# Up-projections of two MLPs as 2x2 block products in seven block multiplications instead of eight

## The chip, the cores and the metric

The kernel runs on one core of one Trainium2 chip. The metric is the device time of one launch in microseconds. The kernel before took 1144.09 us, the median of three runs (1143.23 to 1144.69).

## What is computed

A decoder trunk of four sub-layers on x of 1 x 512 x 1024, in float32: an mLSTM mixer, an MLP, a short gated convolution, an MLP. RMS norms stand before and after each sub-layer, and the result is added to the residual stream.

```python
def layer(x, g, mixer):                  # for each of the four sub-layers
    return x + rms_norm(mixer(rms_norm(x, g_pre)), g_post)

def mlp(x, w_up, w_down):                # D_MODEL 1024, D_FF 4096
    return jnp.square(jax.nn.relu(x @ w_up)) @ w_down
```

Both MLPs have weights of their own (w_mlp_up 1024 x 4096, w_mlp_down 4096 x 1024). The other two mixers have projections of the same kind, which the change touches only in how their activations are stored.

## The kernel before

**Precision.** Every projection is done with each float32 operand split into a high and a low part of type float32r. `split` (L77) makes them: ScalarE casts the high part (L78), VectorE subtracts it from the source for the low part (L79). `mm3` (L101) then issues three matrix products on TensorE, high x high (L104), high x low (L105) and low x high (L106), all accumulated in PSUM. A block product thus needs the high part for its first two instructions, and the low part from the third on.

**Layout.** The normalised activations are turned over on TensorE (L216), four transposes to a PSUM bank, and split into xT0 and xT1. A row tile of 128 tokens is called t = 0 to 3.

**An MLP** (`mlp`, L727). The 4096 columns of the up-projection go in 32 blocks of 128. For each, one DMA brings 1024 x 128 weights (512 KB) into a raw buffer, `split` makes `w` of it, and `proj_T` (L108) does 8 x 3 products of 512 columns (all tokens) into a `pu` bank. `take` (L730) squares the rectified block: ScalarE (L732), VectorE (L734), then a split into `hb`. The first six blocks are done in halves of 256 columns, tokens 0 to 255 first, because `proj_T_many` (L137, STEPS) starts while the last tokens are still in their norm. Four blocks make a group g. `down(g)` (L750) multiplies a group with four row tiles of the down weights: 8 bank-sized results of 12 products of 512 columns. Group 0's are copied to `acc` (L774), the following ones added on VectorE (L776). The order is up, up, down(0), up, down(1) and so on; the last two groups are done together in `last_product` (L243), which also does the post-norm and the tail.

**What sets the order.** Each engine runs its instructions in the order in which they were built, and waits at the first whose operands or buffers are not ready. The builder moves instructions somewhat against the program text. SyncE (SP) issues the DMAs in the same way, in order. Steps with a long chain, the transposes of the last tokens above all, are put off by `put_off` and `step` until so many us of products have been placed ahead of them (LATE, BLOCK).

**The tail of a product** (`tail_to`, L711). `add_normed` adds the normed result to the residual (L231), `pre_norm` squares it on ScalarE (L181), takes a power on GpSimd (L173), scales it on VectorE (L207) and puts off the transposes. For tile t = 3 this chain is open when the next sub-layer's products begin.

**Buffers.** raw 2 and w 9 (weights), hb 8 pairs, xr 4 (the residual, in SBUF all the time), acc 4, xT0 and xT1 of 16 KB per partition; PSUM pu 4 banks, pd 2, pt 2.

Of the kernel before, what the change touches and what calls it, by code (L numbers as in the profile page):

```python
# [14 lines left out]
P = 128  # L15
D = 1024
# [13 lines left out]
NRAW = 2  # L30
WSPLIT = 1
NW = 9
NT2 = 8
LATE = 10.4
BLOCK = 5.2


@with_exitstack
def tile_hybrid_trunk(
# [20 lines left out]
    ps = ctx.enter_context(tc.tile_pool(name="ps", bufs=1, space=bass.MemoryType.PSUM))  # L60

# [22 lines left out]
    def load(src, a, tag="raw", bufs=NRAW):  # L84
        raw = big.tile([P, 1024], F32, tag=tag, name="raw", bufs=bufs)
        nc.sync.dma_start(raw.rearrange("p (a b) -> p a b", a=a), src)
        return raw
# [4 lines left out]
    def halved(raw, a):  # L92
        w = big.tile([P, 2, 1024], F32R, tag="w", name="w", bufs=NW)
        for hs in halves(WSPLIT):
            split(w[:, 0, hs], w[:, 1, hs], raw[:, hs])
        return w.rearrange("p s (a b) -> p s a b", a=a)
# [4 lines left out]
    def mm3(o, lhs, rhs, first, last):  # L101
        lh, ll = lhs
        rh, rl = rhs
        nc.tensor.matmul(o, lh, rh, start=first, stop=False)  # L104
        nc.tensor.matmul(o, lh, rl, start=False, stop=False)  # L105
        nc.tensor.matmul(o, ll, rh, start=False, stop=last)  # L106

    def proj_T(o, w, xT, t0, t1):  # L108
        for ko in range(KO):
            if ko % 2 == 0:  # L110
# [4 lines left out]
                (xT[0][:, t0:t1, ko, :], xT[1][:, t0:t1, ko, :]),  # L115
# [4 lines left out]
    # work for the tensor engine whose operands come through a long chain is put off until  # L120
    # enough matrix products (in us) stand before it
# [54 lines left out]
    def junk(n):  # L176
        return big.tile([P, n], BF16, tag="junk", name="junk", bufs=2)
# [7 lines left out]
    def x_tile():  # L185
        return big.tile([P, H * VA], F32, tag="xr", name="xr", bufs=4)

    def acc_tile():
        return big.tile([P, H * VA], F32, tag="acc", name="acc", bufs=4)

    def new_xT():
        return [
            big.tile([P, NT, KO, P], F32R, tag=f"xT{s}", name=f"xT{s}", bufs=1) for s in range(2)
        ]
# [4 lines left out]
    def pre_norm(t, xt, g, xT, late):  # L199
# [12 lines left out]
        def turn():  # L212
            for q, xn in enumerate(xns):
# [5 lines left out]
                hi = xT[0][:, t, 4 * q : 4 * q + 4, :].rearrange("p k n -> p (k n)")  # L219
                lo = xT[1][:, t, 4 * q : 4 * q + 4, :].rearrange("p k n -> p (k n)")  # L220
                last = split(hi, lo, tp)
# [15 lines left out]
    def hb():  # L237
        return big.tile([P, 2, S], F32R, tag="hb", name="hb", bufs=8)

    def scratch(a, b):  # L240
        return big.tile([P, a, b], F32, tag="w", name="scratch", bufs=NW)

    def last_product(wm, r0, hT, g, tail, accs=None, ends=False):  # L243
        """rows r0 : r0 + D of wm times hT, on top of accs; the post-norm's gain; then the tail"""
# [8 lines left out]
        def ks(o, t, cs, k0, k1):  # L253
            hf, c0 = divmod(cs.start, 512)
            n = cs.stop - cs.start
            for k in range(k0, k1):
# [3 lines left out]
                    (hT[k][:, 0, t * P : (t + 1) * P], hT[k][:, 1, t * P : (t + 1) * P]),  # L260
# [50 lines left out]
    # ---------------------------------------------------------------- mLSTM  # L311
    wi = w_in_mlstm[0]
    xT = new_xT()
    xs = [x_tile() for _ in range(NT)]

    def load_x(t):
        nc.sync.dma_start(xs[t][:, :D], x2[t * P : (t + 1) * P, :])

    # values, token-major, with a column of ones
# [6 lines left out]
    def v_half(hf, ws, before, after):  # L326
        for t in range(NT):
            before(t)
            o = pu()
            for ko in range(KO):  # L330
                if ko % 2 == 0:
# [3 lines left out]
                    (xT[0][:, t, ko, :], xT[1][:, t, ko, :]),  # L335
# [4 lines left out]
            if hf == 0:  # L340
                v[t] = x_tile().rearrange("p (h e) -> p h e", h=H)
                nc.gpsimd.memset(v[t][:, :, DV : DV + 1], 1.0)
# [9 lines left out]
    raws = [load(v_src(0, i), 2, "hb", 8) for i in range(2)]  # L352
    load_x(1)
    raws += [load(v_src(0, i), 2, "hb", 8) for i in range(2, 4)]

    # the first gain is spread over the partitions by a product with ones
# [7 lines left out]
    # the first tokens' way to the tensor engine goes ahead of the weights'  # L364
# [19 lines left out]
    graw = big.tile([P, KO, 2 * H], F32, tag="raw", name="graw", bufs=NRAW)  # L384
# [7 lines left out]
    # gate weights: high parts of the input gates in columns 0:4 and of the forget gates in  # L392
    # columns 32:36, their low parts 64 columns further
    gw = big.tile([P, KO, P], F32R, tag="hb", name="gw", bufs=8)
# [22 lines left out]
    for ko in range(KO):  # L417
        for part in range(2):
# [3 lines left out]
                xT[part][:, :, ko, :],  # L422
# [4 lines left out]
    def take_qk(i, o):  # L427
        h = i // 2
        if i % 2 == 0:
            qk[h] = big.tile([P, 2, S], F32, tag="hb", name="qk", bufs=8)  # L430
# [19 lines left out]
    # gates as rows [head, token]  # L450
    row_tiles = [acc_tile() for _ in range(4)]
    row_i = [0]

    def rows():
        i = row_i[0]
        row_i[0] += 1
        return row_tiles[i // 2][0:H, (i % 2) * S : (i % 2 + 1) * S]
# [58 lines left out]
    # gates as columns [token, chunk, kind, head]  # L516
# [11 lines left out]
    # chunk decays on all partitions  # L528
# [7 lines left out]
    # decay matrices exp(a_s - M_l), zero above the diagonal  # L536
# [11 lines left out]
    DT = scratch(4, S).rearrange("p h (c l) -> p h c l", c=NT)  # L548
# [26 lines left out]
    Pm = scratch(NT, S)  # L575
    kw = scratch(NT, S)
    C = [None] * H
    Cs = [big.tile([P, H, VA], F32, tag="hb", name="C", bufs=8) for _ in range(2)]

    def scores(c):  # L580
        cs = slice(c * P, (c + 1) * P)
        sp = pd()
        for h in range(H):
# [4 lines left out]
            out=Pm[:, c, :].rearrange("p (h l) -> p h l", h=H),  # L588
# [4 lines left out]
        if c < NT - 1:  # L593
            kp = pd()
            for h in range(H):
                nc.tensor.transpose(kp[:, h * P : (h + 1) * P], kT[h][:, cs], ident)
            nc.vector.tensor_tensor(
                out=kw[:, c, :].rearrange("p (h l) -> p h l", h=H),
# [5 lines left out]
    def core(c, hf):  # L604
        cs = slice(c * P, (c + 1) * P)
        if hf == 0:
            comb[c] = acc_tile().rearrange("p (h e) -> p h e", h=H)
# [253 lines left out]
```

## Time and profile before

The profiled execution:

| | value |
|---|---|
| span, first to last instruction | 1141.5 us |
| time of the runs, median | 1144.09 us |
| TensorE busy (PE) | 1130.4 us |
| VectorE busy (DVE) | 547.3 us |
| ScalarE busy (ACT) | 384.9 us |
| HBM read / written | 108.58 / 2.10 MB |

The profile is one execution. PE rows are matrix products, PEld rows weight loads beside them, SP rows DMA issues. A line such as L79 is where the instruction was issued, and where a helper issues for many callers, the tile's name tells them apart. In the groups by line, "x192 | 234.2, 1224 | 205.5" means 192 instructions, 234.2 us busy, 1224 ns for one, and 205.5 us of idle time of that engine just ahead of them, with what ended it. In a timeline the columns are start and duration in us, engine, line and operation; brackets hold the idle time before it and what released it. Listed durations of products overlap, so their rate is read from start to start.

### The profile page before, as it was taken

How to read it: one execution, taken by the hardware profiler on the slowest of the kernel's cores; microseconds unless marked ns; L12 is line 12 of the kernel's file. 1: busy time of each engine (PE TensorE's matmuls, PEld its weight loads, DVE VectorE, ACT ScalarE, POOL GpSimd, SP SyncE). 2: the span in 40 equal slices, each digit the busy share in tenths (PEclk: the TensorE clock that was granted, in tenths of full speed). 3: DMA queues.
4: the chain of work that ended last, by engine and by line, in shares of the span. 5: the costliest groups of instructions: out<-in, count | busy, mean ns of one | idle time of the engine just before them, and what ended most of it. 6: DMA issues, size and time to landing. Idle time of an engine off the chain costs nothing. (4 is left out here: it accounts for less than half of the span.)

```text
span 1141.5 us, 13204 instructions
## 1 busy us (share of the span) xinstructions
PE 1130.4 (99%) x5379; PEld 931.8 (82%) x5379; DVE 547.3 (48%) x773; ACT 384.9 (34%) x620; POOL 50.6 (4%) x85
## 2 busy tenths in 40 slices
PE   8999999999999999999999999999999999999997
PEld 6878887898888888888889888789888888888886
DVE  5643763555235344444375444355624434535423
ACT  6342542444414123133253222144532312313211
POOL 2000010100000000000130000010000000000011
PEclk9999999999999999999999999999999999999999
DMA  6512441154224224133135332205422413314201
GB/s 211 141 64 66 135 160 57 30 163 141 75 73 131 74 91 129 56 111 111 37 92 167 112 93 92 74 3 165 136 78 82 129 56 111 111 57 127 93 18 56
DMA packets 130722, 111.53 MB, mean 98 GB/s; under 512 B 4549, under 2 KB 111333, under 8 KB 130662
## 3 DMA queue, kind: packets, MB, share of 16 engines
q1 hardware_dynamic: 130662, 110.69, 31.3%
q8 instruction: 42, 0.69, 0.3%
q14 instruction: 18, 0.15, 0.0%
HBM read 108.58 MB, written 2.10 MB: 97 GB/s over the span
## 5 line engine op out<-in xcount | busy, mean ns | idle before, releaser
L79 DVE TENSOR_TENSOR w<-raw,w 128x1024 fp32r<-128x1024 f32 x192 | 234.2, 1224 | 205.5 <-ACT w L78 205.5
L78 ACT CAST w<-raw 128x1024 fp32r<-128x1024 f32 x192 | 199.7, 1049 | 379.6 <-issue 181.0
L104 PE MATMUL pu<-xT,w 128*128 128x512 f32 (+1 forms) x880 | 327.6, 372 | 0.0
L105 PE MATMUL pu<-xT,w 128*128 128x512 f32 (+1 forms) x880 | 326.3, 371 | 0.0
L106 PE MATMUL pu<-xT,w 128*128 128x512 f32 (+1 forms) x880 | 325.6, 370 | 0.0
L104 PE MATMUL pd<-w,hb 128*128 128x512 f32 (+1 forms) x648 | 253.7, 391 | 0.3 <-DVE t L278 0.2
L106 PE MATMUL pd<-w,hb 128*128 128x512 f32 (+1 forms) x648 | 253.5, 391 | 0.0
L105 PE MATMUL pd<-w,hb 128*128 128x512 f32 (+1 forms) x648 | 253.5, 391 | 0.0
L104 PEld LDWEIGHTS pu<-xT,w 128*128 128x128 f32 x880 | 165.6, 188 | 30.9 <-issue 0.6
L106 PEld LDWEIGHTS pu<-xT,w 128*128 128x128 f32 x880 | 165.5, 188 | 30.7
L105 PEld LDWEIGHTS pu<-xT,w 128*128 128x128 f32 x880 | 165.6, 188 | 30.4 <-issue 0.2
L104 PEld LDWEIGHTS pd<-w,hb 128*128 128x128 f32 x648 | 121.6, 188 | 29.0 <-DVE t L278 1.2
L105 PEld LDWEIGHTS pd<-w,hb 128*128 128x128 f32 x648 | 121.7, 188 | 27.8
L106 PEld LDWEIGHTS pd<-w,hb 128*128 128x128 f32 x648 | 121.5, 187 | 27.5
L776 DVE TENSOR_TENSOR acc<-acc,pd 128x512 f32<-128x512 f32 x80 | 54.8, 686 | 119.9 <-PE pd L106 119.9
L734 DVE SCALAR_TENSOR_TENSOR t<-pu,t 128x512 f32<-128x512 f32 x60 | 41.3, 688 | 73.7 <-ACT t L732 73.3
L732 ACT ACTIVATE t<-pu 128x512 f32<-128x512 f32 x60 | 35.8, 597 | 99.3 <-PE pu L106 99.0
L79 DVE TENSOR_TENSOR hb<-t,hb 128x512 fp32r<-128x512 f32 x80 | 54.8, 686 | 8.9 <-ACT hb L78 8.9
L78 ACT CAST hb<-t 128x512 fp32r<-128x512 f32 x80 | 49.4, 619 | 21.4 <-DVE t L734 18.1
L284 POOL TENSOR_TENSOR t<-acc,gain 128x512 f32<-128x512 f32 x14 | 18.2, 1300 | 662.6 <-DVE acc L281 347.2
L181 ACT ACTIVATE junk<-acc 128x512 bf16<-128x512 f32 (+1 forms) x17 | 10.3, 607 | 58.8 <-DVE acc L281 57.3
L281 DVE TENSOR_TENSOR acc<-acc,pd 128x512 f32<-128x512 f32 (+1 forms) x17 | 11.1, 655 | 37.3 <-PE pd L106 37.3
(139 smaller groups left out, 684.3 us busy)
## 6 DMA issues: line engine op xcount, KB each, us to landing
raw<-in_w_mlp_up_dram SPq DMA_DIRECT2D x64, 512.0 KB, 4.0
raw<-in_w_mlp_down_dram SPq DMA_DIRECT2D x64, 512.0 KB, 3.5
raw<-in_w_in_mlstm_dram SPq DMA_DIRECT2D x24, 512.0 KB, 4.1
raw<-in_w_in_conv_dram SPq DMA_DIRECT2D x24, 512.0 KB, 3.8
raw<-in_w_out_mlstm_dram SPq DMA_DIRECT2D x8, 512.0 KB, 4.0
raw<-in_w_out_conv_dram SPq DMA_DIRECT2D x8, 512.0 KB, 3.5
xr<-in_x_dram SPq DMA_DIRECT2D x7, 512.0 KB, 3.5
gain<-in_norm_g_dram SPq DMA_DIRECT2D x7, 512.0 KB, 5.0
```

Of the source, the lines that this page charges most:

```text
L78: hi = nc.scalar.copy(dst_hi, src)
L79: lo = nc.vector.tensor_tensor(out=dst_lo, in0=src, in1=dst_hi.bitcast(F32), op=ALU.subtract)
L104: nc.tensor.matmul(o, lh, rh, start=first, stop=False)
L105: nc.tensor.matmul(o, lh, rl, start=False, stop=False)
L106: nc.tensor.matmul(o, ll, rh, start=False, stop=last)
L181: nc.scalar.activation(junk(n), src, AF.Square, scale=float(D) ** -0.5, accum_out=ms[:, i : i + 1])
L281: nc.vector.tensor_tensor(out=y, in0=y, in1=o, op=ALU.add)
L284: eng.tensor_tensor(out=yg, in0=y, in1=g[:, cs], op=ALU.mult)
L732: nc.scalar.activation(r, o, AF.Relu)
L734: nc.vector.scalar_tensor_tensor(out=q, in0=o, scalar=0.0, in1=r, op0=ALU.max, op1=ALU.mult)
L776: nc.vector.tensor_tensor(out=yh, in0=yh, in1=o, op=ALU.add)
```

## The change

**Seven products.** A quad is 512 columns of the up-projection, seen as a 2x2 matrix of weight blocks a, b, c, d (each 512 x 256: a and b from the upper half of the rows, c and d from the lower), times a 2x2 matrix of activation blocks (512 features x 256 tokens). Eight quads make an MLP. In place of eight block products there are seven: X = a·a11, Z = (a+b)·p1, X += c·a12, Y = (b+d)·r3, Z += d·p4, Y += (a+d)·n2, O = (a+c)·a22. Each is 24 products of 256 columns (`prod`). Sums and differences of X, Y, Z and O give the four result blocks, five VectorE operations a quad.

**Activations.** `Seven` replaces xT0 and xT1 for the two MLPs: the seven units a11, a12, p1, r3, p4, n2 and a22, each split into high and low. a11 and a12 come of tiles 0 and 1; the others need tiles 2 and 3, with four VectorE sums for each of them. `Plain` is the layout of the other projections.

**Weights.** Each of the seven products has its own factor: a, c, d as loaded, and a+b, b+d, a+d, a+c summed on VectorE first (each sum 1024 elements per partition). Each is split, so a quad has seven splits instead of four. Its four blocks are read as 512 x 256 in runs of 1 KB. Down weights come as two row tiles of 512 columns in runs of 2 KB instead of whole rows.

**Order.** The first three quads of an MLP are begun together: three X products (`begin`), then three X += (`first_done`), then run(0), run(1), down(0), run(2), down(1), run(3) and so on. The tiles of the last tokens are put ahead with `flush`.

**Buffers.** 15 shared slots of 8 KB (tag u: weight factors, Seven, residual pairs, sums), 4 pairs hb of 16 KB, 7 raw slots of 4 KB (weight blocks, and the values of a quad), in place of the buffers above. The residual is written to DRAM (xd0 to xd3, 512 KB each) by each tile's tail, and read back when group 4's down product has been placed.

```diff
-NRAW = 2
-NW = 9
+NU = 15
+NHB = 4
+NRAW = 7
+AHEAD = 3
...
+    class Seven:
...
+        def take(self, t, q, tp):
...
+            s22, r3, p1 = temp(), temp(), temp()
+            nc.scalar.copy(s22, a)
+            tt(out=p1, in0=self.first, in1=s22, op=ALU.subtract)
+            tt(out=r3, in0=k0, in1=self.first, op=ALU.subtract)
+            self.part("p1", c, p1)
+            self.part("r3", c, r3)
+            tt(out=k0, in0=p1, in1=k0, op=ALU.subtract)
+            tt(out=k1, in0=k0, in1=k1, op=ALU.add)
...
+                pre_norm(t, xs[t], gn, nxt, LATE)
+                if aside:
+                    nc.sync.dma_start(xd[t], xs[t])
...
+        def run(self, begun):
...
+            a, b = self.block(0, 0), self.block(0, 1)
+            if not begun:
+                self.begin(a)
+            ca = self.ca
+            tt(out=a, in0=a, in1=b, op=ALU.add)
+            w = self.factor(a)
+            z = pu()
+            prod(z, w, f["p1"], True)
+            cb = self.values()
+            nc.scalar.copy(cb[:, 1], by_tile(z))
+            if not begun:
+                c = self.block(1, 0)
+                self.first_done(c)
+            d = self.block(1, 1)
+            tt(out=b, in0=b, in1=d, op=ALU.add)
+            w = self.factor(b)
+            y = pu()
+            prod(y, w, f["r3"], True)
+            nc.scalar.copy(cb[:, 0], by_tile(y))
+            w = self.factor(d)
+            tt(out=a, in0=a, in1=d, op=ALU.add)
+            w6 = self.factor(a)
+            prod(z, w, f["p4"], False)
...
+            prod(y, w6, f["n2"], False)
+            tt(out=ca[:, 1], in0=by_tile(y), in1=ca[:, 1], op=ALU.add)
...
+            prod(o, w4, f["a22"], True)
...
-        proj_T_many([(w_up[i], j * P) for j in range(2 * G)], xT, take, 6)
-        down(0)
-        for g in range(1, NG - 2):
-            up(g + 1)
-            down(g)
-        up(NG - 1)
+        flush(2)
+        quads = [quad(g) for g in range(NG)]
+        for qd in quads[:AHEAD]:
+            qd.begin()
+        for qd in quads[:AHEAD]:
+            qd.first_done()
+        flush()
+        for g in range(2):
+            quads[g].run(True)
+        for g in range(NG - 2):
+            down(g)
+            quads[g + 2].run(g + 2 < AHEAD)
+            if g == NG - 4:
+                xs[:] = token_tiles()
+                for t in range(NT):
+                    nc.sync.dma_start(xs[t], xd[t])
```

Three places show how the built order moved. Names carry a number for the buffer's use, and `out<-in` reads from right to left; `u` tiles are weight factors or activations, `raw` tiles blocks or values of a quad, `t` tiles short-lived halves.

First, TensorE at the start of the first MLP. Before, the transposes of tile 3 (t_1874, t_1876) stand in the middle of the up blocks:

```order
L104 MATMUL pu<-xT_1466,w 128x256
L105 MATMUL pu<-xT_1467,w 128x256
L106 MATMUL pu<-xT_1466,w 128x256
L216 MATMUL pt<-ident,t_1874 128x128 x4
L216 MATMUL pt<-ident,t_1876 128x128 x4
L104 MATMUL pu<-xT_1466,w 128x256
```

Of the changed kernel the same place, from the last down-type product of the mixer on; t_1785 and t_1787 are tile 2, t_1895 and t_1897 tile 3:

```order
L118 MATMUL pd<-u,hb 128x512
L278 MATMUL pt<-ident,t_1785 128x128 x4
L278 MATMUL pt<-ident,t_1787 128x128 x4
L278 MATMUL pt<-ident,t_1895 128x128 x4
L116 MATMUL pu<-u 128x256
L117 MATMUL pu<-u 128x256
L278 MATMUL pt<-ident,t_1897 128x128 x4
L118 MATMUL pu<-u 128x256
```

Tile 3's first four transposes moved from behind 90 products of the up-projection to a place ahead of all of them, and its other four to behind two.

Second, ScalarE in the middle of an MLP. Before, the reads of finished blocks (L732) alternate with casts of weights (w) for blocks five places on: w_3913 is the weight of pu_3916.

```order
L732 ACTIVATE t2_3624<-pu_3599 128x512
L78 CAST hb_3628<-t2_3626 128x512
L78 CAST w_3913<-raw_3911 128x1024
L732 ACTIVATE t2_3661<-pu_3636 128x512
L78 CAST w_3950<-raw_3948 128x1024
L78 CAST hb_3665<-t2_3663 128x512
```

Of the changed kernel, one quad; pu_3273 is X, pu_3304 Z, pu_3371 Y, u_3301 the factor a+b, u_3333 the factor c, u_3368 b+d, u_3397 d and u_3401 a+d:

```order
L81 CAST u_3301<-raw_3266 128x1024
L847 COPY raw_3298<-pu_3273 128x512
L866 COPY raw_3329<-pu_3304 128x512
L81 CAST u_3333<-raw_3331 128x1024
L81 CAST u_3368<-raw_3268 128x1024
L81 CAST u_3397<-raw_3365 128x1024
L81 CAST u_3401<-raw_3266 128x1024
L907 ACTIVATE raw_3298<-pu_3273 128x512
```

TensorE's order there is X, Z, X +=, Y, Z +=, Y +=, O. The copy of Z now stands ahead of the cast of c, the factor of X +=.

Third, VectorE early in an MLP. Before, weights' low parts (w) alternate with takes (L734) and their splits (hb):

```order
L734 SCALAR_TENSOR_TENSOR t2_2104<-pu_1914,t2_2102 128x512
L79 TENSOR_TENSOR w_2345<-raw_2343,w_2345 128x1024
L79 TENSOR_TENSOR hb_2106<-t2_2104,hb_2106 128x512
L734 SCALAR_TENSOR_TENSOR t2_2135<-pu_1915,t2_2133 128x512
L79 TENSOR_TENSOR w_2350<-raw_2348,w_2350 128x1024
L79 TENSOR_TENSOR hb_2137<-t2_2135,hb_2137 128x512
```

Of the changed kernel, from run(0)'s last factor (u_2235) to run(1)'s first (u_2307, which is a+b of raw_2302 and raw_2304):

```order
L82 TENSOR_TENSOR u_2235<-raw_2134,u_2235 128x1024
L861 TENSOR_TENSOR raw_2302<-raw_2302,raw_2304 128x1024
L885 TENSOR_TENSOR raw_1938<-pu_2175,raw_1938 128x512
L886 TENSOR_TENSOR raw_2167<-raw_1938,raw_2167 128x512
L888 TENSOR_TENSOR raw_2167<-raw_2167,raw_1938 128x512
L887 TENSOR_TENSOR raw_2167<-pu_2142,raw_2167 128x512
L910 SCALAR_TENSOR_TENSOR raw_2167<-raw_2167 128x512 x2
L893 TENSOR_TENSOR raw_1938<-pu_2266,raw_1938 128x512
L82 TENSOR_TENSOR hb_2292<-raw_2167,hb_2292 128x512 x2
L910 SCALAR_TENSOR_TENSOR raw_1938<-raw_1938 128x512
L82 TENSOR_TENSOR u_2307<-raw_2302,u_2307 128x1024
```

The sum for run(1) stands ahead of run(0)'s result sums and takes, and the low part of that same factor behind them, two of which (raw_2167 at L910 and its split) read results of run(0)'s products.

More of the change, by code (lines that the diff above doesn't have):

```diff
@@ L35 @@
 BLOCK = 5.2
+PROD = 2.86
+AHEAD = 3
 @with_exitstack
@@ L92, in halved @@
     def halved(raw, a):
-        w = big.tile([P, 2, 1024], F32R, tag="w", name="w", bufs=NW)
-        for hs in halves(WSPLIT):
-            split(w[:, 0, hs], w[:, 1, hs], raw[:, hs])
+        w = unit([2, 1024], F32R)
+        split(w[:, 0, :], w[:, 1, :], raw)
         return w.rearrange("p s (a b) -> p s a b", a=a)
@@ L183, in part_ms, with __init__, part, take @@
         )
[L185 to L194, printed above, removed]
+    class Plain:
+        def __init__(self):
+            self.f = [[unit([4, S], F32R) for _ in range(2)] for _ in range(2)]
+        def take(self, t, q, tp):
+            c = slice(t * P, (t + 1) * P)
+            return split(
+                self.f[0][q][:, :, c], self.f[1][q][:, :, c], tp.rearrange("p (k n) -> p k n", k=4)
+            )
+    class Seven:
+        def __init__(self):
+            self.f = {}
+            self.keep = [None, None]
+            self.first = None
+        def part(self, name, c, src):
+            if name not in self.f:
+                self.f[name] = unit([2, 4, 256], F32R)
+            f = self.f[name]
+            split(f[:, 0, :, c], f[:, 1, :, c], src)
+        def take(self, t, q, tp):
+            c = slice((t % 2) * P, (t % 2 + 1) * P)
+            a = tp.rearrange("p (k n) -> p k n", k=4)
+            if t < 2:
+                if t == 0:
+                    self.keep[q] = raw_tile([4, 256])
+                self.part(("a11", "a12")[q], c, a)
+                nc.scalar.copy(self.keep[q][:, :, c], a)
+                return
+            if q == 0:
+                self.first = a
+                return
+            tt = nc.vector.tensor_tensor
+            k0, k1 = (k[:, :, c] for k in self.keep)
+            def temp():
+                return half_kb().rearrange("p (k n) -> p k n", k=4)
+            s22, r3, p1 = temp(), temp(), temp()
[6 more added lines that the diff above has]
+            tt(out=k1, in0=k0, in1=k1, op=ALU.add)
+            self.part("p4", c, k1)
+            self.part("n2", c, k0)
+            self.part("a22", c, s22)
     def halves(n=2):
@@ L706, in tile_hybrid_trunk, with tail_to @@
             core((j - 1) % NT, 0 if j == 0 else 1)
-    xs = [None] * NT
-    def tail_to(gn, nxt):
+    xs = token_tiles()
+    xd = [dram.tile([P, D], F32, name=f"xd{t}") for t in range(NT)]
+    def tail_to(gn, nxt, aside=False):
         def tail(t, yg, ms2):
@@ new lines, in tile_hybrid_trunk, with prod @@
+        load_x(t)
+    xT2 = Seven()
+    last_product(w_out_mlstm[0], 0, hT, gain(0, 1), tail_to(gain(0, 2), xT2, True))
+    def prod(o, fw, fx, first):
+        for p in range(4):
+            step(PROD / 4)
+            for u in range(2):
+                mm3(
+                    o[:, u * 256 : (u + 1) * 256],
+                    [fw[:, i, p, u * P : (u + 1) * P] for i in range(2)],
+                    [fx[:, i, p, :] for i in range(2)],
+                    first and p == 0 and u == 0,
+                    p == 3,
+                )
@@ new lines, in by_tile, with quad, take @@
+    def by_tile(o):
+        return o.rearrange("p (u n) -> p u n", u=2)
+    def mlp(i, xT, gy, tail, ends=False):
+        NG = FF // P // G
+        hs = [None] * (FF // P // 2)
+        def quad(g):
+            def take(nh, half, c, o):
+                j = 2 * g + nh
+                if o is not None:
+                    nc.scalar.activation(c, o, AF.Relu)
+                else:
+                    o = c
+                nc.vector.scalar_tensor_tensor(
+                    out=c, in0=o, scalar=0.0, in1=c, op0=ALU.max, op1=ALU.mult
+                )
+                if hs[j] is None:
+                    hs[j] = pair()
+                split(hs[j][:, 0, half], hs[j][:, 1, half], c)
+            return Quad(w_up[i], g * 512, g * 512 + 256, xT, take)
+        ys = []
+        def down(g):
+            if g == 0:
+                ys.extend(token_tiles())
+            for hf, cs in enumerate(halves()):
+                ws = [
+                    piece(
+                        w_dn[i][r * P : (r + 2) * P, cs].rearrange("(k p) m -> p k m", p=P), 2
+                    )
+                    for r in (g * G, g * G + 2)
+                ]
+                for t in range(NT):
```

201 lines of the change are left out of this document (115 added, 86 removed).

## The prediction

> **What bounds the kernel now.** I read the head of the page first, then the granted clock of the core, then the view by windows.
>
> ```profile
> span 1141.5 us, 13204 instructions
> PE 1130.4 (99%) x5379; PEld 931.8 (82%) x5379; DVE 547.3 (48%) x773; ACT 384.9 (34%) x620; POOL 50.6 (4%) x85
> core 0: 1141.5 us, clock 0.998
> 360.00:420.00 60.00, 60.00 (x260) 48.56 (x259) 26.87 (x34) 16.64 (x22) 0.00 (x0) 1.00 0.31 98
> ```
>
> TensorE is busy for 99% of the span at a granted clock of 0.998. The last row is 60 us from the middle of the first MLP (busy us of PE, PEld, DVE, ACT, POOL; clock, DMA share, GB/s): PE never stops, while VectorE has 33 us free and ScalarE 43. The kernel is the sum of its matrix products, so a change wins by less product time and loses by idle time of PE. The median of the runs is 1144.09 us (1143.23 to 1144.69), 2.6 us above this span. I sum against the span and add 2.6 at the end.
>
> The price of a product is the distance from start to start in the timeline of PE, since the listed durations overlap.
>
> ```profile
> 254.74 0.28 PE L105 MATMUL pu<-xT,w 128*128 128x256 f32 x1
> ...
> 266.37 0.39 PE L104 MATMUL pu<-xT,w 128*128 128x512 f32 x1
> ...
> 277.53 0.40 PE L104 MATMUL pd<-w,hb 128*128 128x512 f32 x1
> ```
>
> Between the first two starts lie 98 products of 256 columns: 11.63/98 = 0.1187 us each. Between the second and the third lie 48 of 512 columns: 11.16/48 = 0.2325; over the down products behind them it is 0.2319, which I use.
>
> **The change: product time.** Before, an MLP's up-projection is 26 blocks of 24 products of 512 columns and 6 blocks in halves (288 products of 256): 26 x 24 x 0.2319 + 288 x 0.1187 = 178.9 us. Afterwards it is 8 quads x 7 block products x 24 products of 256 columns: 1344 x 0.1187 = 159.5 us. That takes 19.4 us off each MLP, 38.8 in all; one quad takes 19.94 us of PE instead of 4 x 24 x 0.2319 = 22.26, a gain of 2.3. The down-projections keep their products. If nothing waits, the span is 1102.7.
>
> **The change: the other engines.**
>
> ```profile
> L79 DVE TENSOR_TENSOR w<-raw,w 128x1024 fp32r<-128x1024 f32 x192 | 234.2, 1224 | 205.5 <-ACT w L78 205.5
> L78 ACT CAST w<-raw 128x1024 fp32r<-128x1024 f32 x192 | 199.7, 1049 | 379.6 <-issue 181.0 <-PE pu L106 53.5 <-DMA raw<-in_w_mlp_down_dram 53.4
> L79 DVE TENSOR_TENSOR hb<-t,hb 128x512 fp32r<-128x512 f32 x80 | 54.8, 686 | 8.9 <-ACT hb L78 8.9
> L734 DVE SCALAR_TENSOR_TENSOR t<-pu,t 128x512 f32<-128x512 f32 x60 | 41.3, 688 | 73.7 <-ACT t L732 73.3
> L774 ACT COPY acc<-pd 128x512 f32<-128x512 f32 x16 | 9.4, 587 | 27.9 <-PE pd L106 27.7
> ```
>
> A quad has seven factor splits (a cast of 1.05 us on ScalarE, then a low part of 1.22 on VectorE), four additions of 1024 elements (priced as a low part), five of 512 (0.69) and four takes (0.69 + 0.69). VectorE gets 8.6 + 4.9 + 3.4 + 5.5 = 22.4 us where it had 4 x 1.22 + 4 x 1.37 = 10.4. With the down product's 10.4 that makes 32.8 of a period of 42.2: on average it fits. The average hides which operation stands behind which, so I walked the built order with these prices and three reaction times:
>
> ```profile
> 286.09 0.59 ACT L774 COPY acc<-pd 128x512 f32<-128x512 f32 x1 [2.20 <-PE pd L106]
> ...
> 228.15 1.05 ACT L78 CAST w<-raw 128x1024 fp32r<-128x1024 f32 x1 [2.98 <-DMA raw<-in_w_mlp_up_dram]
> 229.24 1.23 DVE L79 TENSOR_TENSOR w<-raw,w 128x1024 fp32r<-128x1024 f32 x1 [1.42 <-ACT w L78]
> ...
> 252.33 0.60 ACT L732 ACTIVATE t<-pu 128x512 f32<-128x512 f32 x1 [6.71 <-PE pu L106]
> 252.82 1.04 ACT L78 CAST w<-raw 128x1024 fp32r<-128x1024 f32 x1
> ```
>
> Three groups of 12 down products after 277.53 reach 285.88, and the copy starts 0.21 later. The low part follows its cast by 0.04. From VectorE to PE I take 0.1, between the two. The last pair matters most: a cast that stands behind a read of a product on ScalarE waits for that product, 6.71 us here. It cost nothing, since its weight was for a block several products later.
>
> **Steady quads.** Now the copy of Z stands directly ahead of the cast of c (u_3333, second excerpt), which the very next product on PE needs. From Z's end: 0.21 + 0.59 for the copy + 1.05 for the cast + 0.04 + 1.22 for the low part + 0.1 = 3.2 us to the third product of X+=, less the two that need only the high part (0.24): 3.0 us idle. On VectorE the additions b+d and a+d stand behind that low part and ahead of the low part of b+d: three operations of 1.22, 3.7 us, against the 2.6 + 0.24 of products left: 0.8 idle. In the down product the third group of 512 columns needs one of two banks back from an accumulation that VectorE reaches only after the takes: about 1.0 by the walk. Together 4.7 us idle against 2.3 saved. Bounds per quad: 2.5 (only c's wait, at its shortest) and 7 (the backlog once more).
>
> **The start of an MLP.** T0 is the end of the product ahead of it; the last token tile's norm chain runs there.
>
> ```profile
> 229.79 1.04 PE L216 MATMUL pt<-ident,t 128*128 128x128 f32 x8
> ...
> 241.74 1.29 PE L216 MATMUL pt<-ident,t 128*128 128x128 f32 x8 [0.23 <-DVE t L207]
> ...
> L231 DVE SCALAR_TENSOR_TENSOR xr<-t,small,xr 128x512 f32<-128x512 f32 x31 | 22.0, 748 | 11.0 <-POOL small L173 11.0
> L207 DVE SCALAR_TENSOR_TENSOR t<-xr,small,gain 128x512 f32<-128x512 f32 x30 | 22.4, 785 | 9.4 <-POOL small L173 9.4
> L173 POOL TENSOR_TENSOR small<-small,mhalf 128x1 f32<-128x1 f32 x32 | 17.6, 550 | 193.8 <-DVE small L168 183.7 <-DVE small L172 9.7
> L181 ACT ACTIVATE junk<-xr 128x512 bf16<-128x512 f32 x32 | 20.1, 631 | 17.5 <-DVE xr L231 15.2 <-DMA xr<-in_x_dram 2.3
> ```
>
> Before, tile 3 is transposed 12 us after T0 (229.79), behind products of tiles 0 to 2 that fill all but 0.23. Afterwards its transposes stand ahead of the first product (first order excerpt), and tile 2's sums and splits stand inside its chain on VectorE. From T0: tile 2's transposes 1.0, ScalarE's copy of them 1.8; six operations of 0.69 on VectorE, 6.0; residual 0.75, 6.7; square, sum, power, 8.5; xn, 9.3; three low parts and the other xn, 12.15; low part of the first weight, 13.4. So the first begin ends at 13.5 + 22 x 0.1187 = 16.1, where 4.9 would do. Nine operations of 0.69 stand ahead of the next weight's low part: 21.2, its begin ends at 23.8. ScalarE copies that product before it casts the third weight, so the chain of 3.0 us comes again, and again ahead of the first completion: 29.5 and 35.3; the other two follow without a wait, 40.95. The work in it is 2.1 for four groups of transposes and six block products of 2.85, 19.2: **21.8 us idle**. Bounds: 16 (the last two waits covered) and 28 (the weights' transfers late by 4 and one more chain).
>
> **The first runs.** In run(0) ScalarE's copy of Z and its casts stand behind the takes of three quads: PE waits 3.6, then 0.8. Run(1) pays for the seven raw slots.
>
> ```profile
> raw<-in_w_mlp_up_dram SPq DMA_DIRECT2D x64, 512.0 KB, 4.0
> ```
>
> Its second block is issued when run(0)'s last addition (53.9) frees a slot and lands at 58.0, 4.0 later and a little. VectorE has the sum of it ahead of all of run(0)'s takes (third excerpt), and the low part behind them and the second pass of run(0)'s takes: about twelve operations of 0.69 and 1.22 later, at 67.4, where run(0) ended at 59.6. PE waits 7.7, and Y another 2.7 for a block whose slot came free late. Down(0), run(2) and down(1) add 0.3, 2.8 (an hb pair that down(0) holds) and 1.3. So 4.4 + 10.4 + 4.4 = 19.2; bounds 12 and 24.
>
> Up to down(1) this is 41 us idle. Then three quads at 4.7, quad 6 with four slots given to the reloaded residual, 6.7, and quad 7, 3.7: 24.5. An MLP has **65.5 us idle**, where before had 0.3 at these places.
>
> **Edits costed at nothing.** Four residual stores per MLP stand on SP ahead of begin's second weight; it lands by about 17.5, and ScalarE casts it at 18.9. If the stores hold the queue for longer, up to 4 us more per MLP (in the 28). The four reloads and the down pieces in 2 KB runs lie under a down product of 22 us. The other projections' layout changes addresses only: 0, from -2 to +3 for what I can't see in it.
>
> **The sum.** Per MLP 65.5 - 0.3 - 19.4 = +45.8, both +91.6: span 1233.1, time **1235.7**. Bounds of the idle per MLP: 16 to 28, 12 to 24 and five quads at 2.5 to 7: 40.5 to 87, or 1185 to 1279; the ends hardly fall together, so this case's own range is 1195 to 1270.
>
> **Rivals.** *Only the product time counts.* If the casts were ready when their products come, 38.8 us would go: **1105**. It decides where the idle of one MLP stays under 19.4 us. VectorE's 33 free us of 60 speak for it; against it, a cast behind a copy of Z can't start before Z has ended, and my start alone has 21.8. The Trainium skill ("Perfetto Trace Analysis", "Identifying the Most-Contended Engine") says to optimise the engine of highest occupancy first; by that rule PE, at 99%, gets its 38.8 us, and it leads to this rival. Chance 0.12, with partial forms up to 1140.
>
> *Only the starts cost.* If VectorE's backlog is shorter and the five later quads break even (2.3 idle each), 41 + 11.6 - 19.7 = 32.9 per MLP stay: **1210**; with starts and runs at their low ends (28), 1184. Chance 0.14.
>
> *The clock drops.* After an idle stretch PE could run slower for a while.
>
> ```profile
> 11.18 0.63 PE L104 MATMUL pu<-w,xT 128*128 128x512 f32 x1
> 11.60 0.63 PE L105 MATMUL pu<-w,xT 128*128 128x512 f32 x1
> 12.03 0.63 PE L106 MATMUL pu<-w,xT 128*128 128x512 f32 x1
> ```
>
> At the program's start products of 512 columns are 0.43 apart, not 0.232. Four us at that pace lose 1.8 us. With an idle of 8 us at an MLP's start, one of 7.7 in run(1) and two of 3 to 5 between, four such stretches per MLP add 7, both 15: **1250**; with longer slow stretches 1275. The Trainium skill ("TensorE: Matmul & The Clock Gate", "Part 1: The HAM clock gate") says that one idle window of about 3.4 us halves the clock until a busy window has passed. The start's 0.43 agrees with it; no later gap in this trace is long enough to show it. Chance 0.16.
>
> *The change doesn't do what it says*: seven block products stand in the built order, so no chance of its own.
>
> **Chances.** Forecast 0.55, clock 0.16, starts only 0.14, faster 0.12, within 0.2% 0.03 (2.3 us, about what a measurement of this kernel can tell). The range 1160 to 1275 leaves out the faster cases and thin tails.
>
> **What would show it.** Afterwards PE should be some 130 us idle; waits for ScalarE's high parts (L81) and VectorE's low parts (L82) should lead its list; each steady quad should show 3 us idle ahead of X+=, with periods of 47 us where they were 44.5; the third begin should end 29 us after T0. I am wrong if the gaps ahead of X+= are under 1 us, or if the first begin ends within 8 us of T0.

## The result, and the profile after

The changed kernel takes 1255.66 us, the median of four runs (1252.63 to 1258.14), where the kernel before took 1144.39 (four runs, 1143.23 to 1144.83). The ratio is 1.0973, with a 95% interval of 1.0951 to 1.0995. The forecast was 1235.7.

These lines are the head of the page after, and the granted clock of its core.

```profile
span 1255.6 us, 15249 instructions
PE 1145.9 (91%) x6243; PEld 985.5 (78%) x6243; DVE 733.3 (58%) x993; ACT 449.0 (36%) x692; POOL 50.8 (4%) x85
...
PEclk9999999778999999989999999997899999999999
...
core 0: 1255.6 us, clock 0.955
```

PE was busy for 99% of 1141.5 us at a clock of 0.998; now it is busy for 91% of 1255.6 at 0.955. Its busy time rose although it has less to multiply: the matrix runs slower in places, and all but one of the slices with a 7 or an 8 in the clock's row are the first stretch of an MLP. What PE waits for is in its list of waits (us in total, times, longest):

```profile
PE pu L116 <- ACT u L81: 44.2, 31, 2.7
PE pu L118 <- DVE u L82: 24.8, 23, 5.7
PE pt L278 <- DVE t L269: 19.5, 6, 8.3
PE pd L117 <- DVE u L82: 4.7, 2, 2.3
```

L81 and L82 are the two lines of `split` in this kernel, L116 and L118 the first and the third product of `mm3`. PE waits 31 times for a high part, all but one of them in the MLPs, and 23 times for a low part of an up factor. The third row is the transposes that wait for the last tiles' norm, the fourth two down products late in the MLPs.

The start of the first MLP in the timeline of PE, from the transposes of tile 2 to run(1):

```profile
232.65 1.04 PE L278 MATMUL pt<-ident,t 128*128 128x128 f32 x8
242.03 1.08 PE L278 MATMUL pt<-ident,t 128*128 128x128 f32 x4 [8.35 <-DVE t L269]
...
246.34 0.41 PE L118 MATMUL pu<-u 128*128 128x256 f32 x1
246.56 0.41 PE L116 MATMUL pu<-u 128*128 128x256 f32 x1
...
253.25 0.38 PE L116 MATMUL pu<-u 128*128 128x256 f32 x1 [2.66 <-ACT u L81]
254.51 0.58 PE L118 MATMUL pu<-u 128*128 128x256 f32 x1 [0.76 <-DVE u L82]
...
268.26 0.58 PE L116 MATMUL pu<-u 128*128 128x256 f32 x1 [1.62 <-ACT u L81]
...
285.39 0.39 PE L116 MATMUL pu<-u 128*128 128x256 f32 x1 [2.18 <-ACT u L81]
...
304.22 0.58 PE L118 MATMUL pu<-u 128*128 128x256 f32 x1 [5.68 <-DVE u L82]
```

Tile 3's transposes, without an idle gap of size before, now wait 8.35 us. The products behind them start 0.22 us apart where 0.1187 was the price. The last two rows are Y of run(0) and Z of run(1). A steady quad, at the products of X+= in the same timeline:

```profile
441.94 0.39 PE L116 MATMUL pu<-u 128*128 128x256 f32 x1 [1.68 <-ACT u L81]
...
443.20 0.39 PE L118 MATMUL pu<-u 128*128 128x256 f32 x1 [0.75 <-DVE u L82]
443.42 0.29 PE L116 MATMUL pu<-u 128*128 128x256 f32 x1
...
488.43 0.39 PE L116 MATMUL pu<-u 128*128 128x256 f32 x1 [1.67 <-ACT u L81]
...
489.69 0.58 PE L118 MATMUL pu<-u 128*128 128x256 f32 x1 [0.75 <-DVE u L82]
490.07 0.41 PE L116 MATMUL pu<-u 128*128 128x256 f32 x1
490.28 0.41 PE L117 MATMUL pu<-u 128*128 128x256 f32 x1
```

The period is 46.5 us (441.94 to 488.43), where four blocks and a down product took 44.5 before. In both quads PE waits 1.7 us for c's high part and 0.75 for its low part. After 443.20 the products go on at 0.12; after 489.69 they are 0.21 apart. What ScalarE and VectorE do ahead of 441.94 is in their timelines:

```profile
440.35 0.58 ACT L866 COPY raw<-pu 128x512 f32<-128x512 f32 x1 [2.25 <-PE pu L118]
440.84 1.05 ACT L81 CAST u<-raw 128x1024 fp32r<-128x1024 f32 x1
```

```profile
441.92 1.23 DVE L82 TENSOR_TENSOR u<-raw,u 128x1024 fp32r<-128x1024 f32 x1 [6.41 <-ACT u L81]
```

ScalarE is idle for 2.25 us ahead of the copy of Z, which needs Z's last product; the cast that PE waits for stands behind that copy, and VectorE is idle for 6.41 us ahead of the low part. All three engines wait for one another, while c needed to wait for nothing: SyncE issued the quad's four blocks within the 10.3 us from 406.65 on. The window around it says that neither ScalarE (16.72 of 48 us busy) nor VectorE (30.42) is short of time (the columns as in the prediction's row):

```profile
440.00:488.00 48.00, 43.70 (x267) 38.32 (x265) 30.42 (x36) 16.72 (x21) 0.00 (x0) 1.00 0.28 88
```

**Where the time went.** I summed, over PE's timeline, each start-to-start distance above the product's own price (0.1187 or 0.2319): distances that are longer by over 0.12 us as idle time, the others as slow pace. A product of 512 columns at half pace falls under idle time by this rule, some 3 us after the change. With some missing records, the sums are good to a few us.

| us, first / second MLP | before | after |
|---|---|---|
| tile 2's transposes to the end of the MLP | 361.6 / 366.7 | 419.3 / 420.6 |
| PE idle | 0.4 / 0.6 | 58.0 / 55.7 |
| slow pace | 0.3 / 0.2 | 19.1 / 17.2 |
| products and transposes at full pace | 360.9 / 359.3 | 342.1 / 340.8 |

So 112.7 us of idle time and 35.8 of slow pace came in and 37.3 of work went. The rest of the span, 2.5 us, arose outside the MLPs, ahead of the first one.

### The profile page after: what moved, and what is told of

The parts are those of the page before. It is cut to its first block, busy times and chain, and to the rows that moved or that the text cites. A ratio compares the mean times of both kernels' runs of the same rounds, so it can differ in the third digit from the quotient of the medians.

```text
span 1255.6 us, 15249 instructions
## 1 busy us (share of the span) xinstructions
PE 1145.9 (91%) x6243; PEld 985.5 (78%) x6243; DVE 733.3 (58%) x993; ACT 449.0 (36%) x692; POOL 50.8 (4%) x85
## 4 chain that ended last, share of the span: by engine, by line
PE 76%; DVE 13%; ACT 5%; DMA 3%; issue 2%; POOL 0%; SPq 0%; POOLq 0%; DVEq 0%; ACTq 0%
PE pu L118 13%; PE pu L116 13%; PE pu L117 12%; PE pd L117 11%; PE pd L116 11%; PE pd L118 11%; DVE u L82 5%; ACT u L81 3%; DMA raw<-in_w_mlp_up_dram 1%; DVE raw L910 1%; DMA raw<-in_w_mlp_down_dram 1%; PE pt L278 1%; DVE hb L82 1%; DVE raw L877 1%; DVE raw L871 1%
## 5 line engine op out<-in xcount | busy, mean ns | idle before, releaser
L116 PE MATMUL pu<-u 128*128 128x256 f32 (+1 forms) x1296 | 424.6, 328 | 44.2 <-ACT u L81 44.2
L118 PE MATMUL pu<-u 128*128 128x256 f32 (+1 forms) x1296 | 420.9, 326 | 24.8 <-DVE u L82 24.8
L117 PE MATMUL pu<-u 128*128 128x256 f32 (+1 forms) x1296 | 418.2, 323 | 0.0
L82 DVE TENSOR_TENSOR u<-raw,u 128x1024 fp32r<-128x1024 f32 (+1 forms) x248 | 291.3, 1202 | 178.5 <-ACT u L81 178.2
L81 ACT CAST u<-raw 128x1024 fp32r<-128x1024 f32 (+1 forms) x248 | 247.7, 1034 | 197.2 <-PE pu L118 57.6
L116 PEld LDWEIGHTS pu<-u 128*128 128x128 f32 x1296 | 261.2, 202 | 66.9 <-ACT u L81 51.1
L118 PEld LDWEIGHTS pu<-u 128*128 128x128 f32 x1296 | 260.2, 201 | 45.9 <-DVE u L82 30.9
L117 PEld LDWEIGHTS pu<-u 128*128 128x128 f32 x1296 | 261.0, 201 | 15.5 <-DVE u L82 0.5
L116 PE MATMUL pd<-u,hb 128*128 128x512 f32 (+1 forms) x648 | 256.0, 396 | 5.4 <-DVE u L335 4.5
L117 PE MATMUL pd<-u,hb 128*128 128x512 f32 (+1 forms) x648 | 255.7, 395 | 4.7 <-DVE u L82 4.7
L118 PE MATMUL pd<-u,hb 128*128 128x512 f32 (+1 forms) x648 | 255.0, 394 | 0.0
L116 PEld LDWEIGHTS pd<-u,hb 128*128 128x128 f32 x648 | 122.2, 189 | 34.9 <-DVE u L335 5.4
L117 PEld LDWEIGHTS pd<-u,hb 128*128 128x128 f32 x648 | 122.5, 189 | 33.7 <-DVE u L82 6.6
L118 PEld LDWEIGHTS pd<-u,hb 128*128 128x128 f32 x648 | 122.5, 189 | 28.4
L946 DVE TENSOR_TENSOR u<-u,pd 128x512 f32<-128x512 f32 x80 | 54.6, 684 | 81.4 <-PE pd L118 81.0
L81 ACT CAST hb<-raw 128x512 fp32r<-128x512 f32 x64 | 38.9, 619 | 62.0 <-DVE raw L910 60.4
L198 ACT ACTIVATE junk<-u 128x512 bf16<-128x512 f32 (+1 forms) x49 | 30.6, 624 | 81.6 <-DVE u L335 54.3
L82 DVE TENSOR_TENSOR hb<-raw,hb 128x512 fp32r<-128x512 f32 x64 | 42.6, 683 | 24.4 <-ACT hb L81 24.4
L278 PEld LDWEIGHTS pt<-ident,t 128*128 128x128 f32 x128 | 16.4, 155 | 24.5 <-ACT u L81 17.1
```

What stands on the lines that cost most here:

```text
L81: hi = nc.scalar.copy(dst_hi, src)
L82: lo = nc.vector.tensor_tensor(out=dst_lo, in0=src, in1=dst_hi.bitcast(F32), op=ALU.subtract)
L116: nc.tensor.matmul(o, lh, rh, start=first, stop=False, skip_group_check=True)
L117: nc.tensor.matmul(o, lh, rl, start=False, stop=False, skip_group_check=True)
L118: nc.tensor.matmul(o, ll, rh, start=False, stop=last, skip_group_check=True)
L198: nc.scalar.activation(junk(n), src, AF.Square, scale=float(D) ** -0.5, accum_out=ms[:, i : i + 1])
```

## The experiments

Two causes are set against each other. **Theory W** (order): PE waits because on ScalarE and VectorE the reads of a finished product stand ahead of the cast and low part of the next one's factor. Its rivals are that VectorE simply has too much to do, and that residual stores or blocks come late. **Theory G** (clock): each gap costs more than itself, since the products behind it run at half pace. The times are compared with runs of the kernel before on the same chip.

**fill: zero products in the gaps**

```diff
+    def fill(o, fx, n, first):
+        for k in range(n):
+            ins = nc.tensor.matmul(
+                o[:, 0:256], zw, fx[:, k % 2, k % 4, :], start=first and k == 0, stop=False,
...
+            fill(z, f["p1"], nz, True)
             prod(z, w, f["p1"], True)
```

> The changed kernel with products of a zero weight put on TensorE into the long waits of both MLPs (60 ahead of an MLP's first product, 14 ahead of the next two begins and of the first completion, 45 ahead of run(1)'s Z, 14 ahead of the first three quads' Y, 14 ahead of each later X +=); they add zero or are overwritten. Theory G (idle stretches close the clock, 39 us of products at half pace): the waits stay, products at 0.21 us almost vanish, the mean granted clock goes from 0.955 to above 0.985, and the time falls by 25 to 40 us, to 1216 to 1231. Rival (the slow pace comes from the work itself, whatever stands idle): clock stays near 0.955, time 1256 or longer by what the added products overrun, up to 1270.

Measured: 1230.24 us, ratio 1.0745 (1.0728 to 1.0761). The fills' group, the clock and two rows of the waits:

```profile
L810 PE MATMUL pu<-u,zw 128*128 128x256 f32 x518 | 66.0, 282 | 0.0
```

```profile
core 0: 1229.4 us, clock 0.990
```

```profile
PE pu L118 <- DVE u L82: 14.1, 18, 1.5
PE pu L116 <- ACT u L81: 8.6, 13, 1.5
```

PE has 518 more products, some 61 us of work that nobody needs (518 x 0.1187), and the kernel is 25.4 us below the changed one. Slow pace in the whole kernel falls from 38.5 us to 16.1 and the clock rises from 0.955 to 0.990, where the rival had no change. G holds: the pace belongs to the gaps. It doesn't explain the gaps, whose time stays, now filled.

**c_first, a_early and both: the next factor ahead of the read**

```diff
 # c_first: c's factor and its cast ahead of the reads of X and Z
+                fa = self.factor(a)
+                c = self.block(1, 0)
+                fc = self.factor(c)
+                with tc.issue_after(hi):
+                    self.begin(f=fa)
...
+                with tc.issue_after(hi):
+                    nc.scalar.copy(cb[:, 1], by_tile(z))
 # a_early: three a blocks loaded and split ahead of the last two row tiles
+        if early is not None:
+            early()
         for t in range(2, NT):
...
-            qd.begin()
+            qd.begin(f=fa.pop(0))
```

> The changed kernel, in which the factor c of the five later quads of each MLP is made ahead of X on ScalarE and VectorE, and the reads of Z and X stand behind the casts of c and b+d; the same operations. Theory W (PE waits because of the order in which ScalarE and VectorE run their work): the 2.4 us idle ahead of X += go in all ten quads, with part of the slow products behind them: 24 to 34 us less, 1222 to 1232. Rival R (the two engines are short of time or of buffers in a quad, so the wait comes back at Y or in the down product): within 6 us of 1255.

> The changed kernel, in which the weights of an MLP's three begins are loaded and split before the last two row tiles of the product ahead; the same operations. Theory W: the three X products follow the transposes of tile 2 at once, tile 3's transposes stand behind them, the third begin ends about 10 us after T0 instead of 34; some 6 us of waits remain ahead of the first completion; 11 us of idle and 5 of slow products less per MLP: 1220 to 1228. Rival R: the transfers and splits collide with the norm chain of tiles 2 and 3, or the slots, and the gain comes back as a later first completion: 1245 to 1256.

> Both edits together (c made first in the later quads, begin weights split early). Theory W: the gains add, 1186 to 1204, and the clock above 0.97. Rival R: less than the larger of the two alone, above 1220.

Measured: c_first 1220.33 us, ratio 1.0651 (1.0626 to 1.0676); a_early 1221.97, 1.0681 (1.0656 to 1.0706); both 1189.23, 1.0390 (1.0375 to 1.0406). PE's timeline of c_first, one quad and the start of the next:

```profile
431.76 0.28 PE L116 MATMUL pu<-u 128*128 128x256 f32 x1
...
451.81 0.39 PE L116 MATMUL pd<-u,hb 128*128 128x512 f32 x1
...
475.09 0.28 PE L116 MATMUL pu<-u 128*128 128x256 f32 x1
```

A quad's 168 products take 20.05 us, 0.1193 each, with no wait inside, and the period is 43.3. Within the quad the seven products do save what the forecast said, once c doesn't stand behind Z: the same work of VectorE fits into a shorter period, so the rival of too much work falls for the steady quads. The period is only 1.2 us under the 44.5 of before, since some 1 us of waiting is left in the down product (one wait there is 0.68 us listed). The time is 2 us below the range that W gave. In a_early the start is what changes:

```profile
231.96 1.04 PE L278 MATMUL pt<-ident,t 128*128 128x128 f32 x8
241.35 0.63 PE L278 MATMUL pt<-ident,t 128*128 128x128 f32 x4
...
247.38 0.58 PE L116 MATMUL pu<-u 128*128 128x256 f32 x1 [3.00 <-ACT u L81]
```

The begins now run between tile 2's transposes and tile 3's, of which the first four wait for nothing and the other four 1.75 us; the first completion still waits 3.00. Slow pace falls with the gaps, to 30.7 us in c_first and 29.9 in a_early. The gains, 35.3 and 33.7, are 69.0 together, and both gains 66.4: two places of one cause, nearly independent of each other.

**pin: Z's copy in the begun quads too**

```diff
             prod(z, w, f["p1"], True)
+            d = self.block(1, 1)
             cb = self.values()
...
-            d = self.block(1, 1)
             tt(out=b, in0=b, in1=d, op=ALU.add)
             w = self.factor(b)
+            if begun:
+                with tc.issue_after(self.hi):
+                    nc.scalar.copy(cb[:, 1], by_tile(z))
```

> The kernel of the run before (both edits), and in the three begun quads too the copy of Z stands behind the cast of b+d on ScalarE; the same operations. Theory W: the waits ahead of Y in run(0) to run(2), 2.1 to 2.8 us each in six quads, go, some 14 us with their refills, and a few slow products: 1168 to 1178. Rival R (raw slots, not the order, hold b+d up): within 4 us of 1189.

Measured: 1158.17 us, ratio 1.0116 (1.0096 to 1.0137), a gain of 31 on both, more than W's price. Idle time falls by 17 us and slow pace from 25.5 to 13.7: the waits ahead of Y in the first three runs are gone, and half-pace stretches with them. The edit has a second part that its expectation doesn't name: in every quad, block d now asks for its raw slot ahead of the values cb. The two parts were not run apart. In the later quads, where only the second part is new, waits of 0.44 to 0.71 us in four down products are down to at most 0.25, which speaks for a share of its own. The longest wait that is left is Z of run(1):

```profile
286.04 0.58 PE L118 MATMUL pu<-u 128*128 128x256 f32 x1 [4.92 <-DVE u L82]
```

**no_stores: the residual not written to DRAM**

```diff
-                if aside:
-                    nc.sync.dma_start(xd[t], xs[t])
...
-                    nc.sync.dma_start(xs[t], xd[t])
+                    load_x(t)
```

> The changed kernel without the eight stores of the residual; the input x is read back in their place, so the output lacks what the sub-layers added. Theory of the forecast (the stores cost nothing, though they stand on SyncE ahead of begin's weights): 1252 to 1258. Rival (they hold up begin's weights): the second begin ends some us earlier in both MLPs, 1240 to 1249.

Measured: 1254.85 us, ratio 1.0961 (1.0939 to 1.0983), against 1.0973 with the stores: no difference, so the stores cost nothing. The reads back stay in this run, so their price isn't tested by it. The traffic of the residual after the change is these two rows of the page (count, KB, us to landing).

```profile
xd<-u SPq DMA_DIRECT2D x8, 512.0 KB, 2.7
u<-xd SPq DMA_DIRECT2D x8, 512.0 KB, 8.3
```

**ahead2_pin, pin_c0, pin_run1, pin_all: what is left of the start**

```diff
 # ahead2_pin: two quads begun, quad 0's c loaded and split early
-AHEAD = 3
+AHEAD = 2
 # pin_c0: tile 3's sums behind both parts of quad 0's c
+                for ins in self.pins:
+                    st.enter_context(tc.issue_after(ins))
 # pin_run1: run(1)'s a+b and its factor ahead of run(0)'s takes
+                with tc.issue_after(nxt.prepare()):
+                    self.finish(ca, cb, y, z, w4)
 # pin_all: the last two
```

> The same, and only two quads are begun at an MLP's start, so that one raw slot more is free, and quad 0's c is split early with the two a. Theory S (run(1) waits because its blocks get raw slots late): the 4.4 to 5.7 us ahead of run(1)'s Z and the 3.5 ahead of the first completion shrink to a third, 10 to 20 us less over both MLPs than the kernel with the pin alone: 1150 to 1165. Rival (the three begun quads are needed as cover for tile 3's chain): a wait of the same size ahead of run(0)'s Z, 1168 to 1180.

> The kernel with the three edits (c first, begin weights early, Z's copy behind b+d's cast), and tile 3's sums and splits stand behind the split of quad 0's c on ScalarE and VectorE; the same operations. Theory W: the 3.0 + 0.5 us ahead of the first completion go in both MLPs, with some slow products: 1148 to 1153. Rival R (c's block lands late, or the wait comes back ahead of run(0)'s Z, which needs tile 3): 1155 to 1160.

> The kernel with the three edits, and run(1)'s sum a+b and its split are made ahead of run(0)'s result sums and takes on VectorE; the same operations. Theory W (the place of that low part behind the takes is the wait): the 5 us ahead of run(1)'s Z go in both MLPs: 1146 to 1150. Theory S (seven raw slots: run(1)'s next block gets its slot only from run(0)'s takes): most of it comes back ahead of run(1)'s Y: 1153 to 1158.

> Both of these edits. Theory W: 1137 to 1143, as fast as the kernel before or faster. Theory S: 1146 to 1152.

Measured: ahead2_pin 1162.07 us (ratio 1.0148, 1.0131 to 1.0165), pin_c0 1160.92 (1.0147, 1.0131 to 1.0163), pin_run1 1160.91 (1.0150, 1.0133 to 1.0167), pin_all 1166.97 (1.0197, 1.0182 to 1.0213). None beats pin. For ahead2_pin that is a miss, though its time lies in the range of theory S: it was to be 10 to 20 us faster than pin. In pin_c0 the wait ahead of the first completion is 0.15 us where pin had 3.00, and longer ones stand ahead of run(0)'s first products, as rival R said:

```profile
245.72 0.58 PE L116 MATMUL pu<-u 128*128 128x256 f32 x1 [0.15 <-ACT u L81]
...
254.47 0.39 PE L116 MATMUL pu<-u 128*128 128x256 f32 x1 [1.97 <-ACT u L81]
...
256.86 0.58 PE L118 MATMUL pu<-u 128*128 128x256 f32 x1 [1.88 <-DVE u L82]
```

In pin_run1 Z of run(1) is ready, and PE stops behind the first two products of Y:

```profile
286.86 0.39 PE L116 MATMUL pu<-u 128*128 128x256 f32 x1 [3.89 <-ACT raw L910]
...
287.93 0.58 PE L118 MATMUL pu<-u 128*128 128x256 f32 x1 [0.52 <-DVE u L82]
```

```profile
286.22 0.59 ACT L910 COPY raw<-pu 128x512 f32<-128x512 f32 x1 [1.24 <-DVE hb L82]
```

In this run's kernel L910 is the copy of Z into cb. The builder put the first products of Z += ahead of the rest of Y, and they add to the bank that this copy reads. The copy itself waits for the low part of one of run(0)'s takes. It writes a raw slot, so I take that slot to be what the take gives free. At 287.93 Y's third product goes on with the low part of b+d, which VectorE has behind run(0)'s takes: without the copy's wait PE would have stopped there until the same time. So one operation put ahead only moves the wait to the next. The times that W gave for pin_c0, pin_run1 and pin_all were all missed, and all three lie above the other case's too, pin_all by 15 us.

**pin_raw8 and raw8_prep: more slots, then the order again**

```diff
 # pin_raw8, from pin
-NRAW = 7
+NRAW = 8
-NT2 = 8
+NT2 = 6
 # raw8_prep: besides, run(1)'s a+b and b+d with their factors ahead of run(0)'s takes
+            tt(out=b, in0=b, in1=d, op=ALU.add)
+            fbd = self.factor(b)
```

> The kernel with the three edits and eight raw slots instead of seven, taken from the short-lived halves (six instead of eight); the same operations. Theory S (raw slots hold the first runs): VectorE can make run(1)'s first low part ahead of run(0)'s takes, its wait of 5 us falls under 2.5 in both MLPs: 1149 to 1154. Rival V (VectorE and ScalarE simply have too much to do between T0 and down(0)): the wait moves on to Y or down(0), 1156 to 1161. Rival T (six halves are too few): 1162 or more.

> The same with eight raw slots, and run(1)'s sums a+b and b+d with their splits made ahead of run(0)'s result sums and takes. Theory S: run(1) starts both Z and Y without a wait over 1 us: 1145 to 1150. Rival V: 1154 to 1161, the wait ahead of Y += or of down(0).

Measured: pin_raw8 1153.72 us, ratio 1.0083 (1.0068 to 1.0099); raw8_prep 1149.80, 1.0056 (1.0042 to 1.0069). Run(1) in the timeline of pin_raw8, then the first completion and run(1)'s Y += in that of raw8_prep:

```profile
281.08 0.39 PE L116 MATMUL pu<-u 128*128 128x256 f32 x1 [0.50 <-ACT raw L899]
...
284.06 0.58 PE L118 MATMUL pu<-u 128*128 128x256 f32 x1 [2.48 <-DVE u L82]
```

```profile
247.92 0.58 PE L116 MATMUL pu<-u 128*128 128x256 f32 x1 [3.05 <-ACT u L81]
...
287.62 0.39 PE L116 MATMUL pu<-u 128*128 128x256 f32 x1 [1.18 <-ACT u L81]
288.89 0.38 PE L118 MATMUL pu<-u 128*128 128x256 f32 x1 [0.76 <-DVE u L82]
```

With one raw slot more (two of the short-lived halves, NT2, make room for it) Z of run(1) no longer waits. What is left of the 4.92 us is 0.50 for the copy of Z (L899 in that kernel) and 2.48 for Y's low part. VectorE sums b+d at 274.24 us, ahead of run(0)'s takes, where pin had it behind them at 286.51, though run(0) itself starts only 3.3 us earlier. So late slots were the reason that the sums came late. In raw8_prep neither Z nor Y of run(1) waits, and 1.18 and 0.76 us stand ahead of Y +=, one of the places that rival V named. The preparation that brought nothing in pin_run1, with b+d besides, brings some 4 us here. Both steps of 4 us are about what the noise of these runs lets one tell; the waits in the timelines are the better evidence. The best version has 38.7 us idle and 13.8 of slow pace behind the program's start, against 4.3 and 2.6 before: 45.6 more, which is over the 38.8 that seven products save. It stays 0.6% slower than the kernel before, and I found none that beats it.

## Why the prediction was right, and where it was off

The direction and the mechanism were right, and the size was 20 us short. (In the front's list of products, the sums are made in place, so the last two factors are a+b+d for Y and a+b+c+d for O; the operations and their prices are the same. An hb pair has 8 KB per partition, not 16.)

- **Product time.** Forecast -38.8 us; the accounting has -37.3 with the transposes, and c_first shows a quad at 20.05 us where the forecast had 19.94. Right.
- **The start.** Tile 3's transposes were put at T0 + 9.3 and came at T0 + 9.4. The chain of waits is nearly the one foretold: the first weight's low part, then copy and cast, three times. The first of these three stands ahead of the second begin (2.66 and 0.76 us), where the forecast had VectorE's backlog alone. Idle time up to Z of run(0) was to be 21.8 us and was 20.2. But each of its steps ended later than forecast (the third begin at T0 + 33.8, not 29.5), since 7.3 us of slow pace came on top.
- **The first runs, down(0) and down(1).** Forecast 19.2 us idle; measured 14.5, and 5.9 of slow pace. Run(1)'s wait for Z was 5.68 instead of 7.7; pin_raw8, where one raw slot more removes it, bears out the cause.
- **Steady quads.** Forecast 3.0 us ahead of X+=, 0.8 ahead of Y and 1.0 in the down product, and a period of 47. Measured 1.83 + 0.92 from start to start (1.68 + 0.75 listed), 0 to 0.38 ahead of Y, no more than 0.6 in all the down products' waits for their bank, and 46.5. c_first shows the cause by undoing it. From quad 3 on the forecast had 24.5 us idle, measured 23.3 in the first MLP, of which two waits of 2.33 in the last two down products were not named apart.
- **The edits costed at nothing.** The stores' 0 is shown by no_stores. For the other projections' layout the bounds were -2 to +3; the 2.5 us outside the MLPs lie in them, and I did not trace them further.
- **The clock.** This is the step that failed. The forecast's own sum had nothing for it, and the rival had four stretches per MLP, 15 us in both, because only gaps like the start's were counted. Measured 35.8. The gaps of the steady quads, too short to count in my pricing, closed the clock in six of ten.

By terms: idle 112.7 us where 130.4 stood (-17.7), slow pace +35.8, product time +1.5 and the part outside the MLPs +2.5. That is 22.1 of the 22.5 by which the span is over the forecast's 1233.1. The two errors had opposite signs, so the total was nearer than its terms, which is luck. The measured time lies nearer to the clock rival's 1250 than to 1235.7. *Only the product time counts* fell with the first row of waits: PE's share of busy time in the page before was 99%, and what decided was the order of two engines that had time to spare. That the best version ends 45.6 us of gaps and pace against 38.8 saved is measured; that a further reordering or more memory could not close it is not shown.

## What to carry to other kernels

A cut in the number of products is worth its price only if each new factor is ready when its product comes: walk the engines that prepare it in the order of their instructions, and look for a read of a finished product ahead of the preparation of the next one. Price a gap of the matrix engine at itself plus the half pace behind it, 1.2 to 1.5 us for each such stretch in the steady quads here, and add up short gaps that lie within some 3.4 us of each other. When an order has been put right and the wait only moves to the next place, look at the buffers: with one more slot a reordering helped that had brought nothing before.

## What the runs showed of the hardware

Short gaps are enough for the half pace. In the ten steady quads the gaps ahead of X+= are 1.83 and 0.92 us within some 3.2 us; in six of them 12 to 16 products at 0.21 us followed (489.69 above), in four none (443.20), with the same gaps. What decides is where the gaps lie. In the changed kernel's trace the granted clock changes only at points of a grid of 3.41 us behind the program's start. These rows are windows of that grid at the two quads shown above (the first time behind the comma is PE's busy time, the third number from the end the clock):

```profile
438.46:441.87 3.41, 1.80 (x16) 1.60 (x14) 0.00 (x0) 1.52 (x2) 0.00 (x0) 1.00 0.00 0
441.87:445.28 3.41, 2.59 (x19) 2.38 (x20) 3.36 (x3) 0.98 (x3) 0.00 (x0) 1.00 0.00 0
...
486.25:489.66 3.41, 1.01 (x7) 0.59 (x5) 1.25 (x2) 1.53 (x2) 0.00 (x0) 1.00 0.00 0
489.66:493.07 3.41, 3.38 (x16) 3.38 (x17) 3.41 (x4) 2.27 (x3) 0.00 (x0) 0.50 0.00 0
```

In the first quad the two gaps fall into two windows, PE is idle for 1.61 us of one and 0.82 of the next, and the clock stays at 1.00. In the second both lie in one window, PE is idle for 2.40 of its 3.41 us, and the next window has a clock of 0.50. The traces of the changed kernel and its twelve variants tell the same: behind the program's start, at full clock, every window with over 1.92 us of idle PE was followed by half clock, none with under 1.59, and between these both occur. So what counted here is the idle time within one window, from about half of it on, and not the longest gap; the listed ends of products are modelled, so this limit is rough.

The Trainium skill ("TensorE: Matmul & The Clock Gate", "HAM oscillation — how this bites in real kernels") describes a clock that is closed again at every DMA wait of a loop and asks for no idle gap over some 3.4 us. In "Part 1: The HAM clock gate" the Trainium skill says that the window that is watched runs freely. The half pace (0.21 against 0.1187 us) and the free window of 3.41 us agree. The limit doesn't: ahead of X+= no single gap is over 1.83 us, nor both together over 2.75, and six of ten closed the clock.
